# Two of seven products take both activation parts in one 512-column matmul

## The chip, the cores and the metric

The kernel runs on one core of one Trainium2 chip. The metric is the device time of one launch in microseconds (us); lower is better. Three executions before the change took 1091.98, 1092.65 and 1094.2 us, median 1092.65. The engines are called as the profile calls them: PE (matrix products, with its weight loads as PEld), DVE and ACT (elementwise work, both can read PSUM, the eight 512-column accumulator banks that PE writes), POOL, SP, and DMA.

## The reference

One transformer-like layer on 512 tokens of width 1024, all in float32. The products that matter here are the dense ones:

```
def swiglu(x, w1, w3, w2):
    return (jax.nn.silu(x @ w1) * (x @ w3)) @ w2

f = swiglu(rms_norm(h, ffn1_pre_g), ffn1_w1, ffn1_w3, ffn1_w2)      # 1024 -> 2816 -> 1024
h = h + 0.5 * rms_norm(f, ffn1_post_g)
u = rms_norm(h, mix_pre_g)
q, k, v, xr, xg = jnp.split(u @ w_in, splits, axis=-1)
...                                                # recurrence, attention
g = jax.nn.sigmoid(u @ w_gate + b_gate)            # two gates
h = h + rms_norm(merged @ w_o, mix_post_g)
f = swiglu(rms_norm(h, ffn2_pre_g), ffn2_w1, ffn2_w3, ffn2_w2)
```

The result must be right to nearly float32, while PE multiplies in a rounded format (fp32r).

## The kernel before, in words

**Three matmuls per product.** Each operand is split into a rounded part `hi` and a remainder `lo` (`split2`: ACT writes hi, DVE writes lo = x - hi). A product is then hi*hi + lo*hi + hi*lo: three matmuls that accumulate into one PSUM bank. In `mm_s`, for each of four 128-deep steps k, L1009 multiplies the weights' hi by the activations' hi, L1010 the weights' lo by the activations' hi, L1011 the weights' hi by the activations' lo, each 256 columns wide. A `mm_s` is twelve matmuls.

**Jobs of seven products.** `Pairs` (both feed-forward blocks' first layers, w1 and w3), `GeluPairs` (xg and a part of wg) and `GatePairs` (the last of wg) compute a pair of 128-row output tiles with a Strassen-like scheme (Winograd's form): the 2x2 block product takes seven products of 256 columns instead of eight. Their weights are a11, a12, a22 and sums s1 to s4; their activations b11, b21, b22 (quarters of the normalized activations, which lie in the tile `uT`, hi and lo of one k 16 KB apart in a partition) and sums t1 to t4, kept in tiles `Xh` and `Xl`. There are 47 jobs: 18 in the first feed-forward (w1a, w3a), 6 in `GeluPairs`, one in `GatePairs`, 22 in the second feed-forward (w1b, w3b). In six of these last ones ("heads", `HEAD_JOBS`) the products a11*b11 and a12*b21 were already made earlier, so a head job has five.

**One job's banks.** A job takes three banks, of which it uses 256 of 512 columns: `bu` gathers a11*b11, then s2*t2, s3*t3, a22*t4 on top; `bx` gathers s1*t1 and then s4*b22; `bc` holds a12*b21. After each step something is copied out: ACT copies bu to `q1` after a11 (L1137), bx to `q5` after s1 (L1140), bu to `u` after s2 (L1148), bu to `v` after s3 (L1172). DVE adds bc + q1 (L1161, in `c11`), bx + u (L1166) and v + q5 (L1173). The product a22*t4 of a job is issued inside the next job, between s1 and s2 (`last`).

**What sets the order.** The program writes each engine's queue out in the order of the Python code, and each engine works through its queue in that order, waiting on semaphores where it needs another engine. Between the products, `prep(n + 1, i)` splits the next job's weights (L230 on ACT, L231 on DVE) and makes the sums of the weights (L1043 to L1045 on DVE, L1082 on ACT and a DMA on POOL); `raws` starts the weight loads on SP's queue. The feed-forward's second layers (`Halves`, L878 to L880, 512 columns) follow straight behind the last job of a stage. Outside of the jobs, `mm_feat` (L241 to L243) does ordinary products.

Of the kernel before, what the change touches and what calls it, by code (L numbers as in the profile page):

```python
# [12 lines left out]
AF = mybir.ActivationFunctionType  # L13
ALU = mybir.AluOpType

P = 128
# [35 lines left out]
def hybrid_layer(ctx: ExitStack, tc: tile.TileContext, a: dict, out: bass.AP):  # L52
# [949 lines left out]
    def mm_s(wa, x, ps, more=False, mark=True, ks=range(4)):  # L1002
# [9 lines left out]
        if mark:  # L1012
            point()

    class Pairs:


# [98 lines left out]
        def run(self, tail, hooks={}):  # L1116
            X = self.X
            assert st["get"] == st["split"] == self.k0, (st, self.k0)
            st["get"] = st["split"] = self.k0 + 2 * len(self.jobs)
            last = silu = lambda: None  # L1120
            far = 3 if self.sums else 2
            for n, (nm, f) in enumerate(self.jobs):
                W = self.w.pop(n)
                first = nm == self.na
                tmp = slot([P, 4, 256], name="ct")
                q1, q5, u, v = (tmp[:, i, :] for i in range(4))
                head, soon = n in self.heads, (2, 3, 4, 4) if n + 1 in self.heads else (1, 2, 3, 4)
                c = self.heads.pop(n) if head else slot([P, 2, SEQ], name="cc")
                if first:
                    self.c1[f] = c  # L1130
                bu, bx, bc = (bank("c")[:, :256] for _ in range(3))
                at = lambda i: [f() for f in hooks.get((n, i), ())]
                if head:
                    act.activation(bu, c[:, 1, :256], AF.Copy)
                else:
                    mm_s(W["a11"], X["b11"], bu)
                    act.activation(q1, bu, AF.Copy)  # L1137
                at(1)
                mm_s(W["s1"], X["t1"], bx)
                act.activation(q5, bx, AF.Copy)  # L1140
                at(2)
                if self.R is not None:
                    self.prep(n + 1, 1)
                silu = last() or silu
                self.prep(n + 1, soon[0])
                mm_s(W["s2"], X["t2"], bu, True)
                del W["s1"], W["s2"]
                act.activation(u, bu, AF.Copy)  # L1148
                at(3)
                if n == len(self.jobs) - 1:  # L1150
                    silu()
                    silu = lambda: None
                    if self.R is None:
                        tail()
                self.prep(n + 1, soon[1])
                at(4)

                def c11():
                    mm_s(W["a12"], X["b21"], bc)
                    del W["a11"], W["a12"]  # L1160
                    dve.tensor_tensor(out=c[:, 0, :256], in0=bc, in1=q1, op=ALU.add)  # L1161

                if n < len(self.jobs) - 1 and not head:
                    c11()
                mm_s(W["s4"], X["b22"], bx, True)
                dve.tensor_tensor(out=c[:, 0, 256:], in0=bx, in1=u, op=ALU.add)  # L1166
                self.prep(n + 1, soon[2])
                silu()
                silu = lambda: None
                mm_s(W["s3"], X["t3"], bu, True)  # L1170
                del W["s3"], W["s4"]
                act.activation(v, bu, AF.Copy)  # L1172
                dve.tensor_tensor(out=c[:, 1, 256:], in0=v, in1=q5, op=ALU.add)  # L1173
                if n == len(self.jobs) - 1:
                    tail()
                    if self.R is not None:
                        tail()
                    c11()
                if not first:
                    c1 = self.c1[f]  # L1180
                    to = self.hid.f
                    to.update((f + i, self.hid.place(f + i, c1[:, i, :])) for i in range(2))
                    dve.tensor_tensor(out=to[f], in0=c1[:, 0, :], in1=c[:, 0, :], op=ALU.mult)
                    dve.tensor_tensor(out=to[f + 1][:, 256:], in0=c1[:, 1, 256:], in1=c[:, 1, 256:], op=ALU.mult)
                self.prep(n + 1, soon[3])
                [self.prep(j, 0) for j in range(n + 2, n + far + 1)]
                self.raws(n + far + 1)

                def last(W=W, bu=bu, c=c, f=f, first=first):
                    mm_s(W.pop("a22"), X["t4"], bu, True)  # L1190
                    if first and self.R is not None:
                        act.activation(c[:, 1, :256], bu, AF.Copy)
                        dve.tensor_tensor(out=c, in0=c, in1=self.R, op=ALU.mult)
                        return lambda: act.activation(c, c, AF.Silu)
                    if first:
                        act.activation(c[:, 1, :256], bu, AF.Silu)
                        act.activation(c[:, 0, :], c[:, 0, :], AF.Silu)
                        act.activation(c[:, 1, 256:], c[:, 1, 256:], AF.Silu)
                    else:
                        c1 = self.c1.pop(f)  # L1200
                        dve.tensor_tensor(out=self.hid.f[f + 1][:, :256], in0=bu, in1=c1[:, 1, :256], op=ALU.mult)

            last()

    class GeluPairs(Pairs):
# [6 lines left out]
        def run(self, scans, yh, yl, tail, gz, bias):  # L1212
# [6 lines left out]
            for n, (nm, f) in enumerate(self.jobs):  # L1219
# [4 lines left out]
                c = slot([P, 2, SEQ], name="g" if gated else "cc")  # L1224
                if gated:
                    gz[f // 2] = c
                bu, bx, bc = (bank("c")[:, :256] for _ in range(3))
                mm_s(W["a11"], X["b11"], bu)
                act.activation(q1, bu, AF.Copy)
                mm_s(W["s1"], X["t1"], bx)  # L1230
                act.activation(q5, bx, AF.Copy)
                self.prep(n + 1, 1)
                last()
                mm_s(W["s2"], X["t2"], bu, True)
# [4 lines left out]
                self.prep(n + 1, 2)  # L1239

                def c11():
                    mm_s(W["a12"], X["b21"], bc)
                    del W["a11"], W["a12"]
                    dve.tensor_tensor(out=c[:, 0, :256], in0=bc, in1=q1, op=ALU.add)

                if n < end:
                    c11()
                mm_s(W["s4"], X["b22"], bx, True)
                dve.tensor_tensor(out=c[:, 0, 256:], in0=bx, in1=u, op=ALU.add)
                parts()  # L1250
                parts = lambda: None
                self.raws(n + 2)
# [49 lines left out]
    class GatePairs(Pairs):  # L1302


        def run(self, gz, bias, tail):
            X, end = self.X, len(self.jobs) - 1
            assert st["get"] == st["split"] == self.k0, (st, self.k0)
            st["get"] = st["split"] = self.k0 + 2 * len(self.jobs)
            for n, (nm, f) in enumerate(self.jobs):
                W = self.w[n]  # L1310
                tmp = slot([P, 4, 256], name="ct")
                q1, q5, u, v = (tmp[:, i, :] for i in range(4))
                c = gz[f // 2] = slot([P, 2, SEQ], name="g")
                bu, bx, bc = (bank("c")[:, :256] for _ in range(3))

                def gate(i, c=c, f=f):
                    act.activation(c[:, i, :], c[:, i, :], AF.Tanh, scale=0.5, bias=bias(f + i))

                mm_s(W["a11"], X["b11"], bu)
                act.activation(q1, bu, AF.Copy)  # L1320
                mm_s(W["s1"], X["t1"], bx, mark=False)
                act.activation(q5, bx, AF.Copy)
                self.prep(n + 1, 1)
                bm = bank("c")[:, :256]
                mm_s(W["a22"], X["t4"], bm)
                mm_s(W["s2"], X["t2"], bu, True)
                act.activation(u, bu, AF.Copy)
                self.prep(n + 1, 2)
                mm_s(W["s4"], X["b22"], bx, True)
                dve.tensor_tensor(out=c[:, 0, 256:], in0=bx, in1=u, op=ALU.add)  # L1330
                self.prep(n + 1, 3)
                if n == end:
                    tail()
                mm_s(W["a12"], X["b21"], bc, mark=False)
                dve.tensor_tensor(out=c[:, 0, :256], in0=bc, in1=q1, op=ALU.add)
                mm_s(W["s3"], X["t3"], bu, True, mark=False)
                W.clear()
                gate(0)
                act.activation(v, bu, AF.Copy)
                dve.tensor_tensor(out=c[:, 1, 256:], in0=v, in1=q5, op=ALU.add)  # L1340
                dve.tensor_tensor(out=c[:, 1, :256], in0=bm, in1=v, op=ALU.add)
                if n < end:
                    self.prep(n + 1, 4)
                    self.prep(n + 2, 0)
                self.raws(n + 3)
                gate(1)

            tail()
# [99 lines left out]
    s4 = small(NT, "s4")  # L1448
# [742 lines left out]
NG = 2  # L2191
NC2 = 0
HEAD_JOBS = (2, 4, 6, 8, 12, 16)
S1_AT = (6, 10, 14, 17)


# [52 lines left out]
```

## Time and profile before

The profiled execution took 1092.45 us, its span from the first to the last instruction is 1090.7 us.

| | busy us | share of the span |
|---|---|---|
| PE | 1082.3 | 99% |
| DVE | 912.3 | 84% |
| ACT | 747.9 | 69% |
| POOL | 215.6 | 20% |

The stages on the span's time line: first feed-forward jobs about 50 to 232 us, its second layer 232 to 334, recurrence, gates, keys and queries to 531 (with the `GeluPairs` jobs from about 472), attention to 660 and the `GatePairs` job at 660 to 670, output products to 776, second feed-forward jobs 776 to 980, its second layer to the end.

Two things have to be known to read the rows. A matmul's duration in the profile is from its start to its modelled end, and matmuls overlap: the time that one adds to PE is the distance from its start to the next one's start. And a row of groups gives: line, engine, operation, output tile<-input tiles, shape, count | busy us, mean ns | idle time just before and what ended it.

### The profile page before, as it was taken

The numbers are of one execution on the slowest core, as the hardware profiler recorded it, in microseconds if no ns is written. First come the engines' busy times: TensorE is split into PE (matmuls) and PEld (weight loads), VectorE is DVE, ScalarE is ACT, GpSimd is POOL, SyncE is SP. The second block draws the span as 40 slices with busy tenths as digits, with TensorE's granted clock in tenths as the row PEclk, the third lists the DMA queues.
The fourth block names the chain that finished last, engine by engine and source line by source line (L and its number), as shares of the span: only waits on it lengthen the run. The fifth ranks groups of instructions, "written<-read, shape, count | busy, mean of one in ns | idle before, by whom it ended". The sixth has DMA issues, their size and how long they took to land.

```text
span 1090.7 us, 18471 instructions
## 1 busy us (share of the span) xinstructions
PE 1082.3 (99%) x6928; PEld 984.8 (90%) x6928; DVE 912.3 (84%) x1463; ACT 747.9 (69%) x1313; POOL 215.6 (20%) x273
## 2 busy tenths in 40 slices
PE   9999999999999999999999999999999999999997
PEld 7899999998889877999988888888999999998886
DVE  4888888889998998889588787777988878789996
ACT  7766656588777778767676666467766666678872
POOL 0013510032101623000144333121100000103200
PEclk9999999999999999999999999999999999999999
DMA  9356775389875743534422357699755555549923
GB/s 324 136 153 143 175 172 121 116 179 233 232 186 181 187 129 104 201 88 109 155 78 78 97 184 195 153 308 228 212 180 146 145 145 146 134 102 243 211 77 135
DMA packets 65530, 177.72 MB, mean 163 GB/s; under 512 B 6544, under 2 KB 10512, under 8 KB 65440
## 3 DMA queue, kind: packets, MB, share of 16 engines
q1 hardware_dynamic: 42128, 122.23, 32.5%
q0 software_dynamic: 23024, 53.79, 26.2%
q8 instruction: 54, 0.88, 0.3%
q10 hardware_dynamic: 288, 0.52, 0.2%
q14 instruction: 36, 0.29, 0.1%
HBM read 160.80 MB, written 13.62 MB: 160 GB/s over the span
## 4 chain that ended last, share of the span: by engine, by line
PE 99%; DMA 0%; DVE 0%; ACT 0%; issue 0%; DVEq 0%; SPq 0%; ACTq 0%
PE c L1009 14%; PE c L1010 14%; PE c L1011 14%; PE f L241 8%; PE f L242 8%; PE f L243 8%; PE hw L878 7%; PE hw L880 7%; PE hw L879 7%; PE pt L1924 1%; PE hw L259 1%; PE hw L261 1%; PE hw L260 1%; PE s L1888 1%; PE s L1887 1%; PE tr L367 1%
## 5 line engine op out<-in xcount | busy, mean ns | idle before, releaser
L1009 PE MATMUL c<-Xh,whi 128*128 128x256 f32 x552 | 156.4, 283 | 0.0
L1010 PE MATMUL c<-Xh,wlo 128*128 128x256 f32 x552 | 156.2, 283 | 0.0
L1010 PE MATMUL c<-uT,wlo 128*128 128x256 f32 x516 | 146.0, 283 | 0.0
L1011 PE MATMUL c<-uT,whi 128*128 128x256 f32 x516 | 146.0, 283 | 0.0
L1009 PE MATMUL c<-uT,whi 128*128 128x256 f32 x516 | 146.0, 283 | 0.0
L1011 PE MATMUL c<-Xl,whi 128*128 128x256 f32 x480 | 135.8, 283 | 0.0
L231 DVE TENSOR_TENSOR wlo<-S,whi 128x1024 fp32r<-128x1024 f32 x94 | 114.5, 1220 | 23.7 <-ACT whi L230 23.7
L241 PE MATMUL f<-uT,whi 128*128 128x512 f32 (+1 forms) x296 | 109.6, 370 | 0.0
L242 PE MATMUL f<-uT,wlo 128*128 128x512 f32 (+1 forms) x296 | 108.6, 367 | 0.0
L243 PE MATMUL f<-uT,whi 128*128 128x512 f32 (+1 forms) x296 | 108.5, 366 | 0.0
L1009 PEld LDWEIGHTS c<-Xh,whi 128*128 128x128 f32 x552 | 106.0, 192 | 0.5 <-ACT S L1082 0.3
L1010 PEld LDWEIGHTS c<-Xh,wlo 128*128 128x128 f32 x552 | 106.0, 192 | 0.0
L230 ACT ACTIVATE whi<-S 128x1024 fp32r<-128x1024 f32 x94 | 95.8, 1052 | 7.9 <-DVE S L1044 3.8
L1010 PEld LDWEIGHTS c<-uT,wlo 128*128 128x128 f32 x516 | 99.1, 192 | 0.1
L1009 PEld LDWEIGHTS c<-uT,whi 128*128 128x128 f32 x516 | 99.1, 192 | 0.1
L1011 PEld LDWEIGHTS c<-uT,whi 128*128 128x128 f32 x516 | 99.1, 192 | 0.0
L1011 PEld LDWEIGHTS c<-Xl,whi 128*128 128x128 f32 x480 | 92.2, 192 | 0.0
L880 PE MATMUL hw<-whi,uT 128*128 128x512 f32 x228 | 88.7, 389 | 0.0
L878 PE MATMUL hw<-whi,uT 128*128 128x512 f32 x228 | 88.7, 389 | 0.0
L879 PE MATMUL hw<-wlo,uT 128*128 128x512 f32 x216 | 84.0, 389 | 0.0
L241 PEld LDWEIGHTS f<-uT,whi 128*128 128x128 f32 x296 | 55.8, 189 | 10.5 <-issue 1.4
L243 PEld LDWEIGHTS f<-uT,whi 128*128 128x128 f32 x296 | 55.8, 189 | 9.1
(479 smaller groups left out, 3117.9 us busy)
## 6 DMA issues: line engine op xcount, KB each, us to landing
raw_w1b<-in_w1b_dram SPq DMA_DIRECT2D x22, 512.0 KB, 4.7
raw_w3b<-in_w3b_dram SPq DMA_DIRECT2D x22, 512.0 KB, 4.6
raw_w3a<-in_w3a_dram SPq DMA_DIRECT2D x21, 512.0 KB, 5.5
raw_w1a<-in_w1a_dram SPq DMA_DIRECT2D x20, 512.0 KB, 5.8
raw_w2a<-in_w2a_dram SPq DMA_DIRECT2D x17, 512.0 KB, 5.7
raw_wg<-in_wg_dram SPq DMA_DIRECT2D x16, 512.0 KB, 4.2
raw_w2a<-in_w2a_dram POOLq DMA_DIRECT2D x15, 512.0 KB, 10.2
raw_w2b<-in_w2b_dram SPq DMA_DIRECT2D x15, 512.0 KB, 6.9
```

Of the source, the lines that this page charges most:

```text
L230: act.activation(hi, src, AF.Copy)
L231: dve.tensor_tensor(out=lo, in0=src, in1=f32(hi), op=ALU.subtract)
L241: pe.matmul(ps[:, c0:c1], wh[:, s], h_, start=k == 0 and c0 == 0, stop=False, skip_group_check=True)
L242: pe.matmul(ps[:, c0:c1], wl[:, s], h_, start=False, stop=False, skip_group_check=True)
L243: pe.matmul(ps[:, c0:c1], wh[:, s], l_, start=False, stop=k == KT - 1, skip_group_check=True)
L259: pe.matmul(acc[n], x[:, 0, c], wh[:, s], start=first, stop=False, skip_group_check=skip)
L878: pe.matmul(ps, xs[:, 0, j, c], hi[:, j, :], start=start and j == 0, stop=False, skip_group_check=True)
L879: pe.matmul(ps, xs[:, 0, j, c], lo[:, j, :], start=False, stop=False, skip_group_check=True)
L880: pe.matmul(ps, xs[:, 1, j, c], hi[:, j, :], start=False, stop=i == self.G - 1, skip_group_check=True)
L1009: pe.matmul(ps, wh[:, s], xh, start=first, stop=False, skip_group_check=True)
L1010: pe.matmul(ps, wl[:, s], xh, start=False, stop=False, skip_group_check=True)
L1011: pe.matmul(ps, wh[:, s], xl, start=False, stop=k == 3, skip_group_check=True)
```

## The change

A new `mm_2` does a product in eight matmuls instead of twelve. For each k, L1020 multiplies the weights' hi by 512 columns at once: the activations' hi (256 columns) and lo (256 columns) as two runs of `uT`. The results go to the lower and to the upper half of a bank. L1021 adds the weights' lo times the activations' hi to the lower half. The halves are added later. It is used for two of the seven products, s4*b22 and a12*b21, the ones beside a11 whose activations lie in `uT`.

```
+    def mm_2(wa, x, ps, mark=True):
+        wh, wl = wa
+        for k in range(4):
+            s = slice(k * P, (k + 1) * P)
+            pe.matmul(ps.rearrange("p (e c) -> p e c", e=2), wh[:, s], x(slice(0, 2), k), start=False, stop=False, skip_group_check=True)
+            pe.matmul(ps[:, :256], wl[:, s], x(0, k), start=False, stop=k == 3, skip_group_check=True)
+        if mark:
+            point()
...
-                bu, bx, bc = (bank("c")[:, :256] for _ in range(3))
+                two = n >= TWO_FROM[self.R is None]
+                bc, bx, bu = (bank("c") for _ in range(3))
+                bu, lo, up = bu[:, :256], slice(0, 256), slice(256, 512)
                 at = lambda i: [f() for f in hooks.get((n, i), ())]
                 if head:
                     act.activation(bu, c[:, 1, :256], AF.Copy)
+                elif two:
+                    mm_s(W["a11"], X["b11"], bc[:, lo])
+                    act.activation(bu, bc[:, lo], AF.Copy)
                 else:
                     mm_s(W["a11"], X["b11"], bu)
                     act.activation(q1, bu, AF.Copy)
                 at(1)
-                mm_s(W["s1"], X["t1"], bx)
-                act.activation(q5, bx, AF.Copy)
+                mm_s(W["s1"], X["t1"], bx[:, lo])
+                act.activation(q5, bx[:, lo], AF.Copy)
...
                 def c11():
-                    mm_s(W["a12"], X["b21"], bc)
+                    if two:
+                        mm_2(W["a12"], X["b21"], bc)
+                        act.activation(q1, bc[:, up], AF.Copy)
+                    else:
+                        mm_s(W["a12"], X["b21"], bc[:, lo])
                     del W["a11"], W["a12"]
-                    dve.tensor_tensor(out=c[:, 0, :256], in0=bc, in1=q1, op=ALU.add)
+                    dve.tensor_tensor(out=c[:, 0, :256], in0=bc[:, lo], in1=q1, op=ALU.add)
...
-                mm_s(W["s4"], X["b22"], bx, True)
-                dve.tensor_tensor(out=c[:, 0, 256:], in0=bx, in1=u, op=ALU.add)
+                mm_2(W["s4"], X["b22"], bx)
+                dve.tensor_tensor(out=u, in0=bx[:, lo], in1=u, op=ALU.add)
+                dve.tensor_tensor(out=c[:, 0, 256:], in0=bx[:, up], in1=u, op=ALU.add)
...
+TWO_FROM = 0, 1
```

`GeluPairs` and `GatePairs` get the same edits. a11*b11 now gathers in bc, where a12*b21 is added to it; ACT copies it from bc into bu (PSUM to PSUM), so that the other sums can go on there. `TWO_FROM` leaves the first job of the second feed-forward's stage with its old a11 and a12. So 47 products s4 and 40 products a12 change: 87 products, 348 matmuls fewer.

At three places the queues read as follows; the job is one of w3a, in the first feed-forward. On PE, the end of a12*b21 and the beginning of s4*b22, before (c_2378 is bc, c_2377 bx; whi_2279/wlo_2280 are a11 and a12, whi_2340/wlo_2341 are s3 and s4):

```order
1419 L1009 MATMUL c_2378<-uT,whi_2279 128x256
1420 L1010 MATMUL c_2378<-uT,wlo_2280 128x256
1421 L1011 MATMUL c_2378<-uT,whi_2279 128x256
1422 L1009 MATMUL c_2377<-uT,whi_2340 128x256
1423 L1010 MATMUL c_2377<-uT,wlo_2341 128x256
1424 L1011 MATMUL c_2377<-uT,whi_2340 128x256
```

and after, with the beginning of s3*t3 behind it (c_2292 is bc, c_2293 bx, c_2294 bu):

```order
1304 L1020 MATMUL c_2292<-uT,whi_2201 128x512
1305 L1021 MATMUL c_2292<-uT,wlo_2202 128x256
1306 L1020 MATMUL c_2293<-uT,whi_2256 128x512
1307 L1021 MATMUL c_2293<-uT,wlo_2257 128x256
...
1314 L1009 MATMUL c_2294<-Xh_488,whi_2256 128x256
```

Three matmuls of 256 columns have become one of 512 and one of 256; the products stand in the same order.

On ACT, the same job before (ct is the tile of q1, q5, u and v; whi are splits of the next job's weights, w a split of its a22):

```order
215 L1137 ACTIVATE ct_2374<-c_2376 128x256
216 L1140 ACTIVATE ct_2374<-c_2377 128x256
217 L230 ACTIVATE whi_2408<-raw_w3a_331_2117 128x1024
218 L1148 ACTIVATE ct_2374<-c_2376 128x256
219 L230 ACTIVATE whi_2438<-S_345_2236 128x1024
220 L230 ACTIVATE whi_2468<-S_346_2237 128x1024
221 L1172 ACTIVATE ct_2374<-c_2376 128x256
222 L230 ACTIVATE w_378_2486<-raw_w3a_332_2119 128x512
```

and after:

```order
229 L1149 ACTIVATE c_2294<-c_2292 128x256
230 L1155 ACTIVATE ct_2290<-c_2293 128x256
231 L230 ACTIVATE whi_2324<-raw_w3a_331_2045 128x1024
232 L1163 ACTIVATE ct_2290<-c_2294 128x256
233 L230 ACTIVATE whi_2354<-S_345_2158 128x1024
234 L1176 ACTIVATE ct_2290<-c_2292 128x256
235 L230 ACTIVATE whi_2378<-S_346_2159 128x1024
236 L1192 ACTIVATE ct_2290<-c_2294 128x256
237 L230 ACTIVATE w_378_2396<-raw_w3a_332_2047 128x512
```

The copy after a11 goes to bu instead of q1 (L1149 for L1137), and one copy is new (L1176, the upper half of bc), between the splits of the next job's s1/s2 and s3/s4.

On DVE, the same job before (cc is the job's result tile):

```order
236 L231 TENSOR_TENSOR wlo_2439<-S_345_2236,whi_2438 128x1024
237 L1161 TENSOR_TENSOR cc_2375<-c_2378,ct_2374 128x256
238 L1166 TENSOR_TENSOR cc_2375<-c_2377,ct_2374 128x256
239 L231 TENSOR_TENSOR wlo_2469<-S_346_2237,whi_2468 128x1024
240 L1173 TENSOR_TENSOR cc_2375<-ct_2374 128x256
```

and after:

```order
250 L231 TENSOR_TENSOR wlo_2355<-S_345_2158,whi_2354 128x1024
251 L1180 TENSOR_TENSOR cc_2291<-c_2292,ct_2290 128x256
252 L1185 TENSOR_TENSOR ct_2290<-c_2293,ct_2290 128x256
253 L1186 TENSOR_TENSOR cc_2291<-c_2293,ct_2290 128x256
254 L231 TENSOR_TENSOR wlo_2379<-S_346_2159,whi_2378 128x1024
255 L1193 TENSOR_TENSOR cc_2291<-ct_2290 128x256
```

One addition is new (L1185, the lower half of bx into u), ahead of the split of s3/s4; L1180 now needs ACT's new copy.

More of the change, by code (lines that the diff above doesn't have):

```diff
@@ L1226, in run @@
                     gz[f // 2] = c
[L1227 to L1231, printed above, removed]
+                bc, bx, bu = (bank("c") for _ in range(3))
+                bu, lo, up = bu[:, :256], slice(0, 256), slice(256, 512)
+                mm_s(W["a11"], X["b11"], bc[:, lo])
+                act.activation(bu, bc[:, lo], AF.Copy)
+                mm_s(W["s1"], X["t1"], bx[:, lo])
+                act.activation(q5, bx[:, lo], AF.Copy)
                 self.prep(n + 1, 1)
@@ L1241, in c11 @@
                 def c11():
-                    mm_s(W["a12"], X["b21"], bc)
+                    mm_2(W["a12"], X["b21"], bc)
+                    act.activation(q1, bc[:, up], AF.Copy)
                     del W["a11"], W["a12"]
-                    dve.tensor_tensor(out=c[:, 0, :256], in0=bc, in1=q1, op=ALU.add)
+                    dve.tensor_tensor(out=c[:, 0, :256], in0=bc[:, lo], in1=q1, op=ALU.add)
                 if n < end:
                     c11()
-                mm_s(W["s4"], X["b22"], bx, True)
-                dve.tensor_tensor(out=c[:, 0, 256:], in0=bx, in1=u, op=ALU.add)
+                mm_2(W["s4"], X["b22"], bx)
+                dve.tensor_tensor(out=u, in0=bx[:, lo], in1=u, op=ALU.add)
+                dve.tensor_tensor(out=c[:, 0, 256:], in0=bx[:, up], in1=u, op=ALU.add)
                 parts()
@@ L1313, in run @@
                 c = gz[f // 2] = slot([P, 2, SEQ], name="g")
-                bu, bx, bc = (bank("c")[:, :256] for _ in range(3))
+                bc, bx, bu = (bank("c") for _ in range(3))
+                bu, lo, up = bu[:, :256], slice(0, 256), slice(256, 512)
                 def gate(i, c=c, f=f):
                     act.activation(c[:, i, :], c[:, i, :], AF.Tanh, scale=0.5, bias=bias(f + i))
[L1319 to L1322, printed above, removed]
+                mm_s(W["a11"], X["b11"], bc[:, lo])
+                mm_s(W["s1"], X["t1"], bx[:, lo], mark=False)
+                act.activation(bu, bc[:, lo], AF.Copy)
+                act.activation(q5, bx[:, lo], AF.Copy)
                 self.prep(n + 1, 1)
@@ L1328, in run @@
                 self.prep(n + 1, 2)
-                mm_s(W["s4"], X["b22"], bx, True)
-                dve.tensor_tensor(out=c[:, 0, 256:], in0=bx, in1=u, op=ALU.add)
+                mm_2(W["s4"], X["b22"], bx)
+                dve.tensor_tensor(out=u, in0=bx[:, lo], in1=u, op=ALU.add)
+                dve.tensor_tensor(out=c[:, 0, 256:], in0=bx[:, up], in1=u, op=ALU.add)
                 self.prep(n + 1, 3)
@@ L1333, in run @@
                     tail()
-                mm_s(W["a12"], X["b21"], bc, mark=False)
-                dve.tensor_tensor(out=c[:, 0, :256], in0=bc, in1=q1, op=ALU.add)
+                mm_2(W["a12"], X["b21"], bc, mark=False)
+                act.activation(q1, bc[:, up], AF.Copy)
+                dve.tensor_tensor(out=c[:, 0, :256], in0=bc[:, lo], in1=q1, op=ALU.add)
                 mm_s(W["s3"], X["t3"], bu, True, mark=False)
```

## The prediction

> **What bounds the kernel now.** I read the page first: busy shares, granted clock, the chain of work that ended last.
>
> ```profile
> span 1090.7 us, 18471 instructions
> PE 1082.3 (99%) x6928; PEld 984.8 (90%) x6928; DVE 912.3 (84%) x1463; ACT 747.9 (69%) x1313; POOL 215.6 (20%) x273
> PEclk9999999999999999999999999999999999999999
> PE 99%; DMA 0%; DVE 0%; ACT 0%; issue 0%; DVEq 0%; SPq 0%; ACTq 0%
> L1009 PE MATMUL c<-Xh,whi 128*128 128x256 f32 x552 | 156.4, 283 | 0.0
> L878 PE MATMUL hw<-whi,uT 128*128 128x512 f32 x228 | 88.7, 389 | 0.0
> ```
>
> PE is busy for 1082.3 of 1090.7 us at full clock, 99% of the chain is PE's, and no time stands idle before its matmuls. So the end moves with the sum of the matmuls, and with any wait that other engines put into PE. The durations of 283 and 389 ns can't be summed: 6928 of them would exceed the span, since matmuls overlap. What counts is the spacing from start to start, which I take from two stretches without a wait. First the instructions of L1010 between 815 and 960 us, every third matmul of a stretch of 256-column products; the columns are count, duration, first and last start:
>
> ```profile
> L1010 PE MATMUL c<-Xh,wlo x187: 283/283/284, 816.4 to 959.7; 128*128 128x256 f32 x187
> L1010 PE MATMUL c<-uT,wlo x156: 283/283/284, 815.0 to 958.6; 128*128 128x256 f32 x156
> L1010 PE MATMUL c<-uT,w x60: 283/283/283, 820.7 to 951.4; 128*128 128x256 f32 x60
> ```
>
> 403 steps start between 815.0 and 959.7, so 402 steps of three matmuls take 144.7 us: 0.360 us each, **120.0 ns per 256-column matmul**. Then L878, every third matmul of the 512-column products, in two windows:
>
> ```profile
> L878 PE MATMUL hw<-whi,uT x64: 389/389/389, 243.0 to 285.9; 128*128 128x512 f32 x64
> L878 PE MATMUL hw<-whi,uT x42: 389/389/389, 1015.8 to 1043.6; 128*128 128x512 f32 x42
> ```
>
> 63 x 3 spacings take 42.9 us and 41 x 3 take 27.8: 227.0 and 226.0 ns, together **226.6 ns per 512-column matmul**. Doubling the columns adds 106.6 ns, not 120.0: each matmul has a fixed part of 120.0 - 106.6 = 13.4 ns. That fixed part is all that PE can win here, because the change sends the same number of columns through it.
>
> The two widths next to each other, at a boundary of stages in either direction:
>
> ```profile
> 49.77 0.39 PE L243 MATMUL f<-uT,whi 128*128 128x512 f32 x1
> 50.00 0.28 PE L1009 MATMUL c<-uT,whi 128*128 128x256 f32 x1
> 50.12 0.28 PE L1010 MATMUL c<-uT,wlo 128*128 128x256 f32 x1
> ...
> 231.99 0.28 PE L1011 MATMUL c<-Xl,w 128*128 128x256 f32 x1
> 232.11 0.40 PE L878 MATMUL hw<-whi,hx 128*128 128x512 f32 x1
> ```
>
> After 512 columns the next matmul starts 0.23 us on, after 256 columns 0.12 us on, whatever comes next: mixing them costs nothing.
>
> **The change on PE.** A k-step of 3 x 120.0 = 360.0 ns becomes 226.6 + 120.0 = 346.6 ns, 13.4 ns less. 87 products of four steps are 348 steps: 348 x 13.4 ns = **4.7 us less** (4.5 to 4.9 with 227.0 or 226.0 ns). The trace has no matmul whose 512 columns lie in two runs 16 KB apart. If the second run started like a matmul of its own, it would take 2 x 120.0 = 240 ns and the gain would be nothing; if runs don't matter, 226.6. DVE gives the nearest row:
>
> ```profile
> L719 DVE TENSOR_TENSOR hEO<-hEO,hEO x30: 674/682/685, 101.3 to 1029.9; 128x512 f32<-128x512 f32 x30
> ...
> L1183 DVE TENSOR_TENSOR hEO<-cc,cc 128x512 f32<-128x512 f32 x20 | 13.7, 684 | 0.1
> ```
>
> L719 works on two runs of 256 columns (the halves that `x()` in `Halves` takes of a tile's two rows), L1183 on 512 in a row, and they take 682 and 684 ns. I take 226.6. The results stay in one contiguous bank.
>
> [...]
>
> **The change on DVE and ACT.**
>
> ```profile
> L1161 DVE TENSOR_TENSOR cc<-c,ct 128x256 f32<-128x256 f32 x34 | 14.2, 416 | 0.0
> L1166 DVE TENSOR_TENSOR cc<-c,ct 128x256 f32<-128x256 f32 x40 | 16.7, 418 | 0.0
> L1137 ACT ACTIVATE ct<-c 128x256 f32<-128x256 f32 x34 | 13.0, 382 | 4.2 <-PE c L1011 3.6
> L1134 ACT ACTIVATE c<-cc x6: 379/379/380, 794.3 to 921.0; 128x256 f32<-128x256 f32 x6
> L230 ACT ACTIVATE whi<-S 128x1024 fp32r<-128x1024 f32 x94 | 95.8, 1052 | 7.9 <-DVE S L1044 3.8
> 815.00:899.70 84.70, 84.70 (x709) 84.70 (x708) 70.06 (x104) 53.75 (x96) 7.75 (x9) 1.00 0.52 144
> ```
>
> DVE gets one addition like L1166 per job: 47 x 0.418 = 19.6 us. ACT gets one copy per a12: 40 x 0.382 = 15.3 us; the copy into bu replaces that into q1, and since L1134 writes PSUM in 0.379 us against 0.382, I price the exchange at nothing. On the path all of this would cost 35 us; it is off the path as long as PE's operands still come in time. The last row is a window with its busy times (PE, PEld, DVE, ACT, POOL): DVE is idle for 14.6 of 84.7 us, in some nine jobs, so about 1.6 us per job; ACT has 31 us, over 3 us per job. 0.42 and 0.38 us fit in.
>
> Order matters too. s2 must wait until ACT has filled bu; before, it waited for ACT's read of bu (L1137) at the same place, with s1 and mostly a22 between (12 or 24 x 0.120 = 1.4 or 2.9 us). Nothing is added. The new copy L1176 waits for a12*b21, and behind it on ACT stands the split of the next job's s3/s4; that is needed a whole job later. DVE's L1180 waits for L1176, but DVE has a split of 1024 columns before it, which takes longer than the copy. No step moves past a DMA.
>
> What counts, then, are the places where PE's operand comes late already. I looked for the shortest time between the end of a split and the matmul that reads it. First a head job, where only five products cover the preparation (DVE, then PE):
>
> ```profile
> 885.61 0.42 DVE L1201 TENSOR_TENSOR hEO<-c,cc 128x256 f32<-128x256 f32 x1 [1.10 <-PE c L1011]
> 888.01 1.22 DVE L231 TENSOR_TENSOR wlo<-raw_w3b,whi 128x1024 fp32r<-128x1024 f32 x1
> ...
> 889.85 0.28 PE L1010 MATMUL c<-uT,wlo 128*128 128x256 f32 x1
> ```
>
> The split ends at 889.23, PE reads it at 889.85: 0.62 us. The row of L1201 says why adding to DVE does little: DVE had waited 1.10 us for PE's a22 there, so 0.42 us from the job before are swallowed, and this job's own addition stands behind the split. From a22 to the read, PE becomes 4 x 13.4 ns = 0.05 us faster: 0.57 us are left. The tightest, in the job before the last:
>
> ```profile
> 961.85 1.22 DVE L231 TENSOR_TENSOR wlo<-raw_w2b,whi 128x1024 fp32r<-128x1024 f32 x1 [1.69 <-ACT whi L230]
> 965.98 1.22 DVE L231 TENSOR_TENSOR wlo<-raw_w3b,whi 128x1024 fp32r<-128x1024 f32 x1
> 967.61 0.28 PE L1010 MATMUL c<-uT,wlo 128*128 128x256 f32 x1
> ```
>
> 0.41 us; again DVE starts from a wait (1.69 us), and no addition falls between. PE comes 0.11 us earlier, 0.30 are left. Third, the second layer behind the first jobs, where DVE has no such rest:
>
> ```profile
> 291.00 1.06 ACT L452 ACTIVATE bc_mix_pre_g<-bc_mix_pre_g 128x1024 f32<-128x1024 f32 x1 [1.71 <-DMA bc_mix_pre_g<-in_mix_pre_g_dram]
> 298.87 1.22 DVE L196 TENSOR_TENSOR wlo<-raw_w2a,whi 128x1024 fp32r<-128x1024 f32 x1
> 301.05 0.39 PE L260 MATMUL hw<-wlo,hT 128*128 128x512 f32 x1
> ```
>
> The split ends at 300.09, 0.96 us before its use, and hangs on ACT, which waits for a DMA. The last job of the stage puts 0.42 us on DVE and 0.38 on ACT, and PE gains 0.11: at worst 0.9 us, and it just fits. All earlier gains move the whole stage, since its loads and splits are released by PE's own progress. So I add no stall.
>
> **Sum.** Against the profiled execution: 1092.45 - 4.7 = 1087.8 us. Its time is 0.2 us below the median of the three, to which the result is compared: 1092.65 - 4.7 = **1088.0 us**.
>
> **Rivals.**
>
> *A part goes into new waits* (10%). At the six head jobs and the two other places the margins are 0.3 to 0.6 us or nothing. If each lost 0.25 us more than its margin, 8 x 0.25 = 2 us would go: 1090.0. For it: the margins are small. Against: DVE begins from a wait on PE before two of the three kinds.
>
> *Two runs, two starts* (6%). A 512-column matmul over two runs takes 240 ns, and PE gains nothing: 1092.6, no change. For it: no row shows such an operand; against: L719. [...]
>
> *Only a small part of the 13.4 ns goes* (3%), because it hangs on something other than the number of matmuls; with a fifth of it, 0.9 us, 1091.7, still within what can't be told from no change. [...] Against: the fixed part is the same at both widths.
>
> *ACT holds DVE up* (5%), the other side. In a normal job L1180 waits for L1176; if that copy stands behind a split of 1.05 us (L230), DVE loses up to 1.05 + 0.38 = 1.43 us, and with the addition 1.85 per job against 1.6 of rest. The excess of 0.25 us in 40 jobs is 10 us: 1092.65 - 4.7 + 10 = 1098, slower. It decides from a loss of 1.2 us per job on; it becomes slower than before from 1.3 on. For it: DVE's rest is the smallest reserve. Against: DVE's own split of 1.22 us stands ahead of L1180 and covers most of the copy.
>
> **Numbers.** Full gain 76%, 1088.0, own range 1087.2 to 1088.8; the rivals 10, 6, 3 and 5%. Differences under 0.2% (2.2 us) can't be told from no change. Faster by more, below 1090.5, holds in the first and most of the second: 0.85. Same: the two PE rivals and the rest of the second, 0.10. Slower: 0.05. The range from 1087.0 to 1090.7 holds the first and most of the second case.
>
> **What would show it.** Right: L1020 spaced 227 ns to its L1021, and that 120 ns to the next; PE still at 99% of the chain; DVE about 932 us busy and ACT about 763; a stage of jobs between 50 and 232 us shorter by 18 x 8 x 13.4 ns = 1.9 us. Wrong: 240 ns or more after L1020; idle time before PE's weight loads with releaser DVE L231 or ACT; waits of L1180 on ACT that grow with each job.

## The result and the profile after

| | before | after |
|---|---|---|
| median, us | 1092.23 (1091.98 to 1094.2, 13 runs) | 1090.02 (1089.89 to 1090.5, 13 runs) |
| span of the profiled execution, us | 1090.7 | 1088.7 |
| PE / DVE / ACT busy, us | 1082.3 / 912.3 / 747.9 | 1080.8 / 929.7 / 761.2 |

The ratio is 0.9979, with a 95% interval of 0.997 to 0.9987. The gain is 2.2 us where 4.7 were predicted. The page of the changed kernel (span; busy times and instructions; the chain; groups with count, busy time, mean ns and idle time before):

```profile
span 1088.7 us, 17888 instructions
PE 1080.8 (99%) x6580; PEld 967.1 (89%) x6580; DVE 929.7 (85%) x1510; ACT 761.2 (70%) x1353; POOL 214.8 (20%) x273
PE 99%; DVE 0%; ACT 0%; issue 0%; DVEq 0%; POOL 0%; POOLq 0%
L1020 PE MATMUL c<-uT,whi 128*128 128x512 f32 x348 | 125.3, 399 | 0.0
L1021 PE MATMUL c<-uT,wlo 128*128 128x256 f32 x348 | 97.8, 281 | 0.0
```

The 348 matmuls are gone from PE (6928 - 6580), PE is still 99% of the chain, and no time stands idle before L1020 or L1021. The missing 2.5 us are therefore in no wait of PE: the matmuls themselves must stand further apart than counted. The time line of PE shows it, here the products a12*b21 and s4*b22 of one job, with a start in each row:

```profile
64.57 0.40 PE L1020 MATMUL c<-uT,whi 128*128 128x512 f32 x1
64.81 0.28 PE L1021 MATMUL c<-uT,wlo 128*128 128x256 f32 x1
64.92 0.40 PE L1020 MATMUL c<-uT,whi 128*128 128x512 f32 x1
65.17 0.28 PE L1021 MATMUL c<-uT,wlo 128*128 128x256 f32 x1
65.28 0.40 PE L1020 MATMUL c<-uT,whi 128*128 128x512 f32 x1
...
67.41 0.28 PE L1009 MATMUL c<-Xh,whi 128*128 128x256 f32 x1
```

Eight pairs take 67.41 - 64.57 = 2.84 us, where 8 x 346.6 ns = 2.77 were counted and 8 x 360 = 2.88 stood before. From L1020 to its L1021 it is 0.24 us (0.25 once), not 0.227. Over all 348 pairs, by the start times in the trace, the first distance is **236.5 ns** on the mean, and the one from L1021 to the next L1020 is **117.1**. Together with the ends of the products, four pairs take 1415 ns on the mean instead of 4 x 346.6 = 1386. Against 1440 before that is 25 ns for each of 87 products, 2.2 us: the whole measured gain. The rest of PE's time agrees. From the first matmul of the jobs to the start of PE's last matmul it is 1033.55 us before (50.00 to 1083.55) and 1031.38 after (50.23 to 1081.61), 2.17 us less, so nothing else on PE changed by much in sum.

The operands come in time, as before. Of the three tight places the splits and their readers now stand so (DVE, then PE, for each place):

```profile
886.55 1.22 DVE L231 TENSOR_TENSOR wlo<-raw_w3b,whi 128x1024 fp32r<-128x1024 f32 x1
888.37 0.28 PE L1010 MATMUL c<-uT,wlo 128*128 128x256 f32 x1
964.15 1.22 DVE L231 TENSOR_TENSOR wlo<-raw_w3b,whi 128x1024 fp32r<-128x1024 f32 x1
965.73 0.28 PE L1010 MATMUL c<-uT,wlo 128*128 128x256 f32 x1
298.12 1.22 DVE L196 TENSOR_TENSOR wlo<-raw_w2a,whi 128x1024 fp32r<-128x1024 f32 x1
299.68 0.39 PE L260 MATMUL hw<-wlo,hT 128*128 128x512 f32 x1
```

That leaves 0.60, 0.36 and 0.34 us; 0.57, 0.30 and at worst 0.06 had been predicted.

### The profile page after: what moved, and what is told of

It reads as the page before. It is cut to its first block, busy times and chain, and to the rows that moved or that the text cites. A ratio compares the mean times of both kernels' runs of the same rounds, so it can differ in the third digit from the quotient of the medians.

```text
span 1088.7 us, 17888 instructions
## 1 busy us (share of the span) xinstructions
PE 1080.8 (99%) x6580; PEld 967.1 (89%) x6580; DVE 929.7 (85%) x1510; ACT 761.2 (70%) x1353; POOL 214.8 (20%) x273
## 4 chain that ended last, share of the span: by engine, by line
PE 99%; DVE 0%; ACT 0%; issue 0%; DVEq 0%; POOL 0%; POOLq 0%
PE c L1009 10%; PE c L1010 10%; PE c L1011 10%; PE f L241 8%; PE f L242 8%; PE f L243 8%; PE c L1020 8%; PE hw L878 7%; PE hw L879 7%; PE hw L880 7%; PE c L1021 4%; PE pt L1950 1%; PE hw L261 1%; PE hw L260 1%; PE hw L259 1%; PE s L1914 1%
## 5 line engine op out<-in xcount | busy, mean ns | idle before, releaser
L1009 PE MATMUL c<-Xh,whi 128*128 128x256 f32 x552 | 156.2, 283 | 0.0
L231 DVE TENSOR_TENSOR wlo<-S,whi 128x1024 fp32r<-128x1024 f32 x94 | 114.5, 1219 | 19.8 <-ACT whi L230 19.6
L1020 PE MATMUL c<-uT,whi 128*128 128x512 f32 x348 | 125.3, 399 | 0.0
L241 PE MATMUL f<-uT,whi 128*128 128x512 f32 (+1 forms) x296 | 109.6, 370 | 0.0
L243 PE MATMUL f<-uT,whi 128*128 128x512 f32 (+1 forms) x296 | 108.5, 366 | 0.0
L1009 PEld LDWEIGHTS c<-Xh,whi 128*128 128x128 f32 x552 | 105.4, 191 | 2.6 <-ACT S L1092 0.3
L230 ACT ACTIVATE whi<-S 128x1024 fp32r<-128x1024 f32 x94 | 98.6, 1055 | 8.3 <-DVE S L1054 4.3
L1021 PE MATMUL c<-uT,wlo 128*128 128x256 f32 x348 | 97.8, 281 | 0.0
L878 PE MATMUL hw<-whi,uT 128*128 128x512 f32 x228 | 88.7, 389 | 0.0
L1020 PEld LDWEIGHTS c<-uT,whi 128*128 128x128 f32 x348 | 65.6, 188 | 13.8
L1021 PEld LDWEIGHTS c<-uT,wlo 128*128 128x128 f32 x348 | 65.9, 189 | 0.0
L241 PEld LDWEIGHTS f<-uT,whi 128*128 128x128 f32 x296 | 55.9, 189 | 10.4 <-issue 1.4
L243 PEld LDWEIGHTS f<-uT,whi 128*128 128x128 f32 x296 | 55.8, 189 | 9.2
L242 PEld LDWEIGHTS f<-uT,wlo 128*128 128x128 f32 x296 | 55.9, 189 | 8.6
L1934 POOL TENSOR_SCALAR P<-P,d 128x256 f32<-128x256 f32 (+1 forms) x64 | 37.7, 607 | 68.3 <-DVE d L1932 44.2
```

The source lines that it names most:

```text
L231: dve.tensor_tensor(out=lo, in0=src, in1=f32(hi), op=ALU.subtract)
L241: pe.matmul(ps[:, c0:c1], wh[:, s], h_, start=k == 0 and c0 == 0, stop=False, skip_group_check=True)
L242: pe.matmul(ps[:, c0:c1], wl[:, s], h_, start=False, stop=False, skip_group_check=True)
L243: pe.matmul(ps[:, c0:c1], wh[:, s], l_, start=False, stop=k == KT - 1, skip_group_check=True)
L878: pe.matmul(ps, xs[:, 0, j, c], hi[:, j, :], start=start and j == 0, stop=False, skip_group_check=True)
L1009: pe.matmul(ps, wh[:, s], xh, start=first, stop=False, skip_group_check=True)
```

## The experiments: the operand, and the work beside PE

The open question was what makes 512 + 256 columns take 354 ns. The first theory was the prediction's own rival, *two runs*: the break in the moving operand costs 10 ns. Its variants were that the distance of the runs (16 KB) or their number matters. Against them stood that the added work on DVE and ACT, or the new use of the banks, takes time from PE (*not hidden*).

**One run.** L1020 reads 512 columns in a row, hi of both token halves, in place of hi and lo of one half; what the upper half gathers is then not hi*lo, so the products of a12 and s4 are wrong.

```
-x(slice(0, 2), k)                     # uT[:, 0:2, 4*hh+k, 256*th : 256*th+256]
+x("two", k)                           # uT[:, 0, 4*hh+k, :]
```

> The 512-column matmul L1020 of the changed kernel is spaced 236.5 ns (226.6 expected), its L1021 117.5. Here its moving operand is one run of 512 columns (the hi part of both token halves, so s4*b22 and a12*b21 are computed with wrong activations); all else as in the change. Theory 'break': the change from one run to the next inside the operand costs the time: the pair falls from 354.0 to 346.6 ns, 348 x 7.4 = 2.6 us less than the change, about 1087.4 us. Rival 'output': writing 512 columns and then 256 into one bank's lower half costs it, whatever is read: 236.5 and 117.5 ns stay, about 1090.0 us. Rival 'distance' (the 16 KB between the runs): as 'break'.

1090.11 us, ratio to the kernel before 0.9976 (0.9967 to 0.9986), span 1088.5. The row of L1020 reads as in the changed kernel, with the same 125.3 us and 399 ns; the distances are 236.5 and 117.1 ns. The break costs nothing.

**Two runs close together, and four runs.** In the first, the two runs are hi of neighbouring k, 2 KB apart; in the second, four runs of 128 columns. Both compute the products of a12 and s4 from other activations, so these are wrong again. The right-hand sides below are what L1020 reads, shortened from the code.

```
+uT[:, 0, 4*hh + k//2*2 : 4*hh + k//2*2 + 2, 256*th : 256*th+256]           # near runs
+uT[:, 0:2, 4*hh + k//2*2 : 4*hh + k//2*2 + 2, 256*th : 256*th+128]         # four runs
```

> Two runs of 256 columns that lie 2 KB apart instead of 16 KB (the hi parts of two neighbouring k, wrong activations for the two products). 'break': nothing changes against the change, L1020 236.5 ns and L1021 117.5, about 1090.0 us. 'distance': 226.6 and 120.0 ns, about 1087.4 us. 'output': as 'break'.

> 512 columns in four runs of 128 (hi and lo of two neighbouring k, wrong activations for the two products). 'break': three breaks instead of one, so the pair of L1020 and L1021 goes from 346.6 + 7.4 to 346.6 + 22.2 = 368.8 ns, 348 x 14.8 = 5.2 us more than the change, about 1095 us, slower than the kernel before. 'output' and 'distance': 354.0 ns, about 1090.0 us.

1089.94 and 1090.43 us in one execution each, spans 1088.2 and 1088.6, distances 236.5 and 117.1, 236.4 and 117.2 ns. Neither the distance nor the number of runs matters on the operand; the output of these products is contiguous in each of these runs.

**Three matmuls in the new arrangement.** The change with all its additions and copies, but each k-step as three matmuls of 256 columns, hi*lo into the upper half; in short:

```
-L1020: 512 columns (hi | lo) into both halves;  L1021: wl * hi into the lower
+wh * hi into the lower;  wl * hi into the lower;  wh * lo into the upper       # 256 columns each
```

> The changed kernel with the three 256-column matmuls of before: hi*hi and lo*hi into the bank's lower half, hi*lo into its upper half. DVE's and ACT's added work, the new waits and the bank order stay, PE's gain is gone; the result is the same. Theory 'hidden' (all of the added work is off the path): every spacing 120.0 ns, 1092.2 us, within 0.3 of the kernel before. Rival 'side work' (part of the missing 2.5 us went into DVE, ACT or waits): 1093 to 1094.7 us, and idle time before PE's weight loads.

1092.86 us, ratio 1.0004 (0.9994 to 1.0013). On its page PE has its old number of matmuls, and DVE and ACT have the change's work:

```profile
span 1091.1 us, 18558 instructions
PE 1082.4 (99%) x6928; PEld 985.0 (90%) x6928; DVE 930.0 (85%) x1510; ACT 761.7 (70%) x1353; POOL 214.8 (20%) x273
```

All distances inside the products are 120.0 ns, and from the first matmul of the jobs to PE's last one it is 1033.66 us, against 1033.55 in the kernel before. The additions, copies, waits and the use of the halves thus cost PE about 0.1 us by the trace; the medians alone could hide up to 1.4 us. The effect of the change lies in the pair of 512 and 256 columns.

## The experiments: the order of the widths

Left were theories on the pair itself: *alternation* (each going from one width to the other and back costs some 7 ns), *the wide one itself* (236.5 in this place whatever follows), *output* (the halves are written in an unlucky order), *another weight tile*.

**Four and four, two and two.** The same eight matmuls in another order, W for 512 columns and N for 256: W W W W N N N N, and W W N N W W N N. The sums computed are the same. In short:

```
 for k in range(4): L1020(k); L1021(k)                     # the change
+for k in range(4): L1020(k)                               # four and four
+for k in range(4): L1021(k)
+for j in (0, 2): L1020(j); L1020(j+1); L1021(j); L1021(j+1)   # two and two
```

> The same eight matmuls of each of the 87 paired products in another order: the four 512-column ones first, then the four 256-column ones; the numbers computed are the same sums. In the changed kernel the pair took 236.5 + 117.1 ns where 226.6 + 120.0 were counted, 7.4 ns more on the mean of its two steps with the 117.1 to 119.0 at the ends. 'Alternation' (each going from one width to the other and back costs those 7 ns): 226.6 ns between two L1020s, 120.0 between two L1021s, the 7 ns once in a product instead of four times, 87 x 3 x 7 ns = 1.8 to 1.9 us less than the changed kernel: about 1088.2 us, span 1086.8, ratio to the kernel before about 0.9962. 'The wide one itself' (a 512-column matmul that adds to a bank in this place takes 236.5 however it is followed): 236.5 ns between two L1020s and 120.0 between two L1021s; 87 x (4 x 236.5 + 4 x 120.0) is 1.0 us more than the changed kernel, about 1091. 'Output': if it is the lower half written twice in a row that costs it, grouping keeps it only where the two groups meet and the time is that of 'alternation'.

> The same eight matmuls again, now as two wide, two narrow, two wide, two narrow. 'Alternation': two goings and comings in a product instead of four, so half the gain of full grouping: 0.9 us below the changed kernel, about 1089.1 us, span 1087.8. 'The wide one itself': 236.5 after every L1020, about 1091. If grouping is worth 1.9 us but this is worth nothing, the price lies in something else than the change of width.

1089.18 us, ratio 0.9964 (0.9952 to 0.9977), and 1088.71 us, ratio 0.9963 (0.9949 to 0.9977). Both medians are below the change's, though the intervals still touch (the change had 0.997 to 0.9987); a run beside it follows below. None of the theories gives these numbers: two and two, with more changes of width, does no worse than four and four. The trace has 1403 ns for a product of four and four and 1394 for two and two. Inside four and four the wide ones are not 226.6 ns apart but 233.3, 235.9, 228.4 and 232.5 in the products of a12, then 117.5, 119.1, 117.5 and 116.6 for the narrow ones. In the products of s4 that follow at once, behind only four narrow ones, the wide ones are 235.0, 233.4, 235.9 and 224.1 ns apart.

**The upper half; the same weights.** Alternating as in the change; in the first L1021 adds to the upper half, in the second it takes the hi weights once more. In the first the sums stay right, since the two halves are added later anyway; the text set down ahead calls them wrong by mistake. The second leaves lo*hi out and adds hi*hi twice, so its products of a12 and s4 are wrong.

```
-pe.matmul(ps[:, :256], wl[:, s], x(0, k), ...)       # the change
+pe.matmul(ps[:, 256:], wl[:, s], x(0, k), ...)       # upper half
+pe.matmul(ps[:, :256], wh[:, s], x(0, k), ...)       # same weights
```

> Alternating as in the changed kernel, but the 256-column matmul adds to the upper half of the bank, where the 512-column one has just written last, instead of the lower (this leaves the lo weights' part in the wrong half: the products of a12 and s4 are computed wrongly). 'Alternation': 236.5 and 117.1 ns as before, span 1088.5. 'Output' (the order in which the halves are written decides): the first or the second of the two spacings moves by several ns, and the span by 348 times that: 7 ns are 2.4 us.

> Alternating as in the changed kernel, but L1021 uses the hi weights that L1020 has just used (the lo weights' part is left out and hi times hi is added twice). 'Alternation': 236.5 and 117.1 ns, span 1088.5. 'Another weight tile' (the 10 ns after the wide one come from where the next weights lie or from loading others than those that stand there): 226.6 ns after L1020, the pair 344 to 347 ns, span 348 x 7 to 10 ns = 2.4 to 3.5 us shorter.

1090.54 and 1090.35 us in one execution each, spans 1088.7 and 1088.6; distances 236.7 and 117.0, 236.5 and 117.1 ns. *Output* and *another weight tile* fall.

**A new theory from the trace of before.** The distances 233, 236, 228, 232 stand there too, to within 1 ns, at all eleven boundaries from 232 us on where 512-column matmuls follow 256-column ones; at least eight narrow ones stand before each. These are the rows that follow the boundary at 232.11 us quoted in the prediction:

```profile
232.35 0.40 PE L879 MATMUL hw<-wlo,hx 128*128 128x512 f32 x1
232.58 0.39 PE L880 MATMUL hw<-whi,hx 128*128 128x512 f32 x1
232.81 0.40 PE L878 MATMUL hw<-whi,hx 128*128 128x512 f32 x1
233.04 0.39 PE L879 MATMUL hw<-wlo,hx 128*128 128x512 f32 x1
233.27 0.39 PE L880 MATMUL hw<-whi,hx 128*128 128x512 f32 x1
233.50 0.39 PE L878 MATMUL hw<-whi,hx 128*128 128x512 f32 x1
233.73 0.39 PE L879 MATMUL hw<-wlo,hx 128*128 128x512 f32 x1
233.95 0.39 PE L880 MATMUL hw<-whi,hx 128*128 128x512 f32 x1
```

From 232.11 to 233.27 five distances take 1.16 us, 232 ns each; the next three take 0.68 us, 227 each. In nanoseconds they are 234, 236, 228, 232, 231, then 227. At 364.76 us, with other tiles (L241 after L243), the first five are 233, 236, 228, 233, 231. On the way back, at 50.00 us, the first two are 114 and 119. So *a transient*: after a run of narrow ones the first five wide ones lose 28 ns in all, and the way back returns about 7; one coming and going costs 21 ns, however much longer the runs are than five.

**Eight in a row.** The products of a12 run their narrow ones first, so that where s4 follows directly the order is N N N N, eight W, N N N N.

```
+a12: for k: L1021(k);  then for k: L1020(k)
+s4:  for k: L1020(k);  then for k: L1021(k)
```

> Products of a12 run their four 256-column matmuls first and the four 512-column ones last, those of s4 wide first, narrow last; where s4 follows a12 (37 places) eight wide ones stand in a row with one coming and going for two products. Same sums. 'Transient': by the trace of the kernel before, after a run of 256-column matmuls the first five 512-column ones are 234, 236, 228, 232 and 231 ns apart and from then on 226.7, and the first after the way back are 114 and 119: some 28 ns lost and 7 given back, 21 ns for one coming and going however long the runs. Then the sixth, seventh and eighth wide one are 226.7 apart, sixteen matmuls take 2 x 1386.4 + 21 = 2794 ns against 2 x 1403 with the two groups of four, 37 x 12 ns = 0.45 us less than four by four: about 1088.7, and about the same as two by two. 'Same price for every wide one' (233 ns on the mean whenever DVE and ACT are busy beside it): 233 to the eighth, 2 x 1403 = 2806 ns, no gain over four by four, 1089.2.

1088.51 us, ratio 0.996 (0.9947 to 0.9973). In the time line of PE, where matmuls of a line that follow each other are merged, the same job's two products (in this file L1022 is the wide one, L1027 the narrow one):

```profile
64.33 0.64 PE L1027 MATMUL c<-uT,wlo 128*128 128x256 f32 x4
64.81 2.00 PE L1022 MATMUL c<-uT,whi 128*128 128x512 f32 x8
66.65 0.64 PE L1027 MATMUL c<-uT,wlo 128*128 128x256 f32 x4
67.12 0.28 PE L1009 MATMUL c<-Xh,whi 128*128 128x256 f32 x1
```

The eight wide ones take 66.65 - 64.81 = 1.84 us; at 233 ns each it would be 1.86. The means over 36 such places are 233.3, 235.8, 228.4, 232.5, 230.8, 226.7, 226.6, 226.7, and back 113.3 and 119.2. The transient stands there step by step and is over with the sixth; sixteen matmuls take 2793 ns, and 2794 were expected.

**Two and two beside the change, and equal widths.** The first two runs are the order W W N N W W N N and the changed kernel itself, timed beside each other. The third splits the 768 columns of a pair as 384 + 384, which computes the products of a12 and s4 wrongly.

```
+pe.matmul(ps[:, :384], wh[:, s], uT[:, 0, 4*hh+k, :384], ...)     # equal widths
+pe.matmul(ps[:, 128:], wl[:, s], uT[:, 0, 4*hh+k, :384], ...)
```

> Two wide, two narrow, two wide, two narrow, timed once more beside the changed kernel itself: its eight matmuls took 1394 ns against 1415, 87 x 21 ns = 1.8 us, so about 1088.4 to 1088.7 where the changed kernel has 1090.0; if the 1088.71 of the first look was the chip, the two come out alike.

> The changed kernel itself beside the other orders: about 1090.0 us, ratio to the kernel before 0.998.

> The 512 + 256 columns of a pair as 384 + 384 (columns 0 to 384 of hi with the hi weights, the same columns with the lo weights into the upper 384 of the bank; the products of a12 and s4 are computed wrongly). 'Change of width': within a product nothing changes, so a step is 160 + 13.4 = 173.4 ns, eight of them 1387 ns and perhaps 10 to 20 ns more at the ends of a product; span about 1086.8 to 1087.5. 'Anything wider than 256 is dearer here' (columns read slower beside the busy DVE and ACT): eight of them 1415 ns as in the changed kernel, span 1088.6.

1088.79 us, ratio 0.9963 (0.9951 to 0.9975); 1090.24 us, ratio 0.9981 (0.9972 to 0.9989); and 1088.18 us in one execution, span 1086.4. Each of the five executions of two and two (1088.38 to 1089.13) is shorter than each of the eleven of the change (from 1089.99 on). The same two products with two and two (L1021 wide, L1023 narrow), then with equal widths:

```profile
64.50 0.63 PE L1021 MATMUL c<-uT,whi 128*128 128x512 f32 x2
64.97 0.39 PE L1023 MATMUL c<-uT,wlo 128*128 128x256 f32 x2
65.20 0.63 PE L1021 MATMUL c<-uT,whi 128*128 128x512 f32 x2
...
67.29 0.28 PE L1009 MATMUL c<-Xh,whi 128*128 128x256 f32 x1
```

```profile
64.79 0.34 PE L1020 MATMUL c<-uT,whi 128*128 128x384 f32 x1
64.97 0.34 PE L1021 MATMUL c<-uT,wlo 128*128 128x384 f32 x1
...
67.40 0.33 PE L1021 MATMUL c<-uT,wlo 128*128 128x384 f32 x1
67.57 0.28 PE L1009 MATMUL c<-Xh,whi 128*128 128x256 f32 x1
```

They take 2.79 and 2.78 us against 2.84 in the changed kernel. With equal widths the distances are 173.4 ns from the fourth matmul on, which is 160 + 13.4: what is wider than 256 is not dearer in this place, only the change of width is.

All orders together, with the mean ns of a product (the change counted 1386.4):

| order | ns per product | median us | ratio to before |
|---|---|---|---|
| three of 256 (new arrangement) | 1440 | 1092.86 | 1.0004 |
| W N W N W N W N (the change) | 1415 | 1090.02, 1090.24 | 0.9979, 0.9981 |
| four and four | 1403 | 1089.18 | 0.9964 |
| eights where a12 and s4 meet | 1398 | 1088.51 | 0.996 |
| two and two | 1394 | 1088.71, 1088.79 | 0.9963 |
| 384 + 384 (wrong sums) | 1391 | 1088.18 (one execution) | |

The ratios of four and four, eights, and two and two can't be told apart by their intervals. From the change to two and two, 87 x 21 ns = 1.9 us were to be had by the trace and 1.5 us were measured beside each other (1090.24 and 1088.79); between the first matmul of the jobs and PE's last one the two traces differ by 1.59 us.

## Why the prediction was half right

**What held.** PE is 99% of the chain before and after. The fixed part of 13.4 ns per matmul is real, and the runs show it at a third width (173.4 ns for 384 columns); all of these distances come from streams with a weight load for every matmul (6928 of each before, 6580 after). That runs in the operand cost nothing was argued from a row of DVE, a weak witness; the operands of one, two and four runs confirm it on PE (236.5, 236.5 and 236.4 ns). That 17.4 us of DVE work (929.7 - 912.3; 19.6 were counted) and 13.3 of ACT work (15.3 counted) are hidden is shown by the three-matmul version: 1.0004 (0.9994 to 1.0013), with 0.1 us more on PE by the trace. The margins at the three tight places held. The window from 815.00 to 899.70 us shows where the work went: DVE is busy for 73.95 us there in place of 70.06, ACT for 55.54 in place of 53.75, and PE still without a gap.

```profile
815.00:899.70 84.70, 84.70 (x650) 81.84 (x649) 73.95 (x113) 55.54 (x104) 7.75 (x9) 1.00 0.52 142
```

**The step that failed** is "mixing them costs nothing", and with it the term of the sum: "348 x 13.4 ns = 4.7 us less" measured 348 x 6.2 ns, about 2.2 us. The step rested on two boundaries and read the distances across them. The first distance behind 232.11 us, 234 ns to the row at 232.35, is too long already, and so are the next four; the rows were in the trace, and the fence ended one row too early. A kernel that goes to the wide ones and back once in a stage loses 21 ns in it. The change made it do so 348 times, and each coming and going took 7 ns of the 13.4 that a pair was to win.

**The marks set ahead.** The measured 1090.02 us lies outside the range that the prediction gave its main case (1087.2 to 1088.8). It lies in the wider one (1087.0 to 1090.7) only because that was stretched for the rival of new waits, which did not come: this part is luck. L1020 stands 236.5 ns before L1021, between the 227 of "right" and the 240 of "wrong". Near to 240, it looked like *two runs, two starts*, and one contiguous run showed that it was not: the size came near, the mechanism was another. The stage of jobs from 50 to 232 us became 0.9 us shorter instead of 1.9 (182.11 us from the first L1009 to the first L878 before, 181.20 after), 144 x 6.2 ns:

```profile
50.23 0.28 PE L1009 MATMUL c<-uT,whi 128*128 128x256 f32 x1
...
231.43 0.40 PE L878 MATMUL hw<-whi,hx 128*128 128x512 f32 x1
```

**The rivals.** *A part goes into new waits* gave 1090.0, almost the measured time, with a cause that is refuted: outside the changed products, the distances on PE that are over 10 ns longer than 120.0, 173.4 or 226.6 ns are too long by 4.5 us in sum, both before and after, and the three-matmul version, with the same added work and copies, takes only 0.1 us more on PE than the kernel before. *Two runs, two starts* is refuted by the single run, which has the same 236.5 ns. *Only a small part of the 13.4 ns goes* had the direction right, but the reason is not that the fixed part hangs on something else; it is there at 256, 384 and 512 columns (120.0, 173.4 and 226.6 ns). The fifth of it was the author's assumption, which no run shows; 6.2 of the 13.4 ns went. *ACT holds DVE up* did not come: before L1180 DVE stands idle for 0.0 us, and 1090.02 us stand against 1098.

## What to carry to other kernels

A price read from long runs of one shape holds for long runs: when a change interleaves two shapes, read more than five instructions behind a boundary in the old trace before calling the boundary free. Where matmuls of two widths have to be mixed, it is worth trying them in pairs or in long runs rather than one by one; with 512 and 256 columns that took the gain from 2.2 to about 3.7 us with the same matmuls. And when a measured size comes near a rival's, undo that rival's cause alone before believing it.

## What was unexpected

After 256-column matmuls, the first five of 512 columns start 233, 236, 228, 232 and 231 ns apart, then 226.7, wherever at least eight of 256 stand before (the first 50 us of the kernel apart), with other tiles and weights too; back at 256 columns, behind eight or more wide ones, the first two take 113 or 114 and 119 or 120. After shorter runs the pattern is another: in the kernel before, behind four wide ones at 660.78 us, the narrow ones are 117, 119, 118, 117, 118 and 119 ns apart. Alternating one by one, the distances are 231 to 242 and 112 to 120. With 384 columns after 256 it is weaker: 177.5, 174.2 and 175.0 before the steady 173.4.

What in PE does this stays open. The runs exclude the shape of the moving operand, the half that is written and the choice of weights (236.4 to 236.7 ns with each of them); that the same distances stand in stages with other work on DVE and ACT speaks against those engines, though no run took their work away. Nor does a fixed price per change explain it: two and two has half the changes of the alternating order but a quarter of its loss (7 against 29 ns a product), since after two wide ones the two narrow ones give back 11.6 or 7.5 ns (the first and the second time in a product), and after a single wide one a narrow one gives back about 3. No run varied the weight loads, which always go with the matmuls here.
